# Second mix of a two-block kernel: convolved tiles interleaved with gate and decay tiles, convolution taps read from PSUM

## The chip, the cores and the metric

The kernel runs on one core of one Trainium2 chip. The metric is the device time of one execution in microseconds, as the median of several runs. Before the change it is 2250.25 us, the median of three runs (2248.23 to 2250.43). The profile is of another execution of the same program.

TensorE multiplies matrices into PSUM (PE in the profile; its weight loads are PEld). VectorE (DVE), ScalarE (ACT) and GpSimd (POOL) work element by element. SyncE (SP) starts the transfers of the weights.

## The reference, cut to what matters

Two blocks follow one another on a sequence of 256 tokens of width 1024. Each is a mixing layer and a lookup among 16384 single-neuron experts. The change lies in the mixing layer of the second block. There one projection `proj = h @ w_in` feeds two recurrences:

```python
qkv = causal_conv_silu(concat(a_q, a_k, a_v), conv_a)        # 4 taps along the tokens, then x * sigmoid(x)
o_a = gated_delta_rule(q, k, v, sigmoid(a_beta), log_alpha)  # 8 heads, chunks of 64 tokens
y_a = (rmsnorm(o_a) * silu(a_gate)) @ w_branch_a
f   = lb + (1 - lb) * sigmoid(b_f)                           # decay
o_b = hgrn2(silu(b_q), 1 - f, b_i, log(f))
y_b = (rmsnorm(o_b) * sigmoid(b_gate)) @ w_branch_b
x   = x + (sigmoid(g_a) * y_a + sigmoid(g_b) * y_b) @ w_out
```

## The kernel before, in words

The projection of the second mix is cut into 80 tiles of 128 channels by 256 tokens. Each tile has its own 512 KB of weights. Weights pass through a ring: SP loads `raw`; ACT rounds it to `hi` (`_conv`, line 152); `lo = raw - hi` is formed by DVE for the first `lo_cut` of 1024 columns and by POOL for the others (line 157). A tile is then 24 matmuls of 128 x 256 (`tile_ch`, line 187), three for each of eight slices of the width: hi by x's high part, hi by its low part, lo by its high part. They add up in one of two PSUM buffers called `mm`. `CUT2 = [384, 640]` gives `lo_cut`: 384 for the first 24 tiles, 640 behind them.

The order of the tiles before is: 24 convolved tiles (for each of 8 heads q, k, v), 8 gate tiles (`a_gate`, written to `sga`), 8 decay tiles (`b_f`, to `fs`), 8 of `b_q` (to `qb`), 8 of `b_gate`, 8 of `b_i`, and 16 for the two mixing gates. Below, tiles count from 0, so the first 40 are tiles 0 to 39.

A convolved tile takes these steps (`conv`, lines 1006 to 1017): ACT copies `mm` to `cvx` (1009), which frees `mm`; ACT makes `cva` from it, scaled by the fourth tap (1011); DVE adds the three other taps, 128 x 255, 254 and 253, with a shift of one to three tokens (1013); ACT takes the sigmoid `cvs` (914); DVE multiplies (1017). Then PE transposes the product (`head`, 1025), and ACT takes sums of squares and copies.

Behind the tiles run generators, which the tile loop advances by two rounds a tile (`after(2)`): `columns` (lines 918 to 1003) makes the decay matrices; `delta(0)` and then `delta(1)` compute the gated delta rule for four heads each; `chain` does the other recurrence (`hgrn`). In `delta`, products on PE (1075) give two matrices; `blocks16` inverts 16 x 16 blocks in a ladder of 15 steps of two DVE instructions (1237, 1238) and writes `X` (1251); three levels follow, each of products on PE (1093, 1094), a mask on DVE (1100), copies on ACT (1104), a product on PE (1110) and a subtraction on DVE (1113); several products end in a transposition (1201) and a product with the gate (1204). Of `hgrn`, the products on DVE are lines 1316 and 1317 and a masked copy is line 1334. Generators take PSUM from six named banks, `y0` to `y3`, `g0` and `g1`, kept in a queue `free` (`bank`, `need`, `done`).

Each engine carries out its instructions in the order in which they stand in its own queue. When the program is built, the framework orders the recorded instructions on each engine by a timeline that it models, so the order on an engine is not simply that of the Python code.

## Time and profile before

| | us |
|---|---|
| median of three runs | 2250.25 (2248.23 to 2250.43) |
| the profiled execution | 2248.88 |
| its span, first to last instruction | 2247.1 |
| PE busy in the span | 2181.1 (97%) |
| DVE busy | 1546.5 (69%) |
| ACT busy | 1166.4 (52%) |
| POOL busy | 829.3 (37%) |

The shares of the whole span say little about one stage. The rows that follow are therefore taken from stretches of the second mix, which starts at about 964 us. Windows give the busy time of each engine in a stretch with the number of its instructions; waits give who waited for whom; the rows of a line give the shortest, median and longest of its instructions. A matmul's record overlaps the next one's, so a count of matmuls in a stretch where PE is never idle gives PE's pace, and their durations do not. A matmul of full 32-bit numbers, as in lines 1025, 1075, 1093 and 1201, stands as two records. A few per cent of the matmul records can be missing.

### The profile page before, as it was taken

How to read it: one execution, taken by the hardware profiler on the slowest of the kernel's cores; microseconds unless marked ns; L12 is line 12 of the kernel's file. 1: busy time of each engine (PE TensorE's matmuls, PEld its weight loads, DVE VectorE, ACT ScalarE, POOL GpSimd, SP SyncE). 2: the span in 40 equal slices, each digit the busy share in tenths (PEclk: the TensorE clock that was granted, in tenths of full speed). 3: DMA queues.
4: the chain of work that ended last, by engine and by line, in shares of the span. 5: the costliest groups of instructions: out<-in, count | busy, mean ns of one | idle time of the engine just before them, and what ended most of it. 6: DMA issues, size and time to landing. Idle time of an engine off the chain costs nothing. (4 is left out here: it accounts for less than half of the span.)

```text
span 2247.1 us, 41435 instructions
## 1 busy us (share of the span) xinstructions
PE 2181.1 (97%) x15512; PEld 2025.8 (90%) x15512; DVE 1546.5 (69%) x3119; ACT 1166.4 (52%) x2210; POOL 829.3 (37%) x626
## 2 busy tenths in 40 slices
PE   8999999999999999988899999999999999999998
PEld 7989999999988888778899898899999999888887
DVE  5659986889544544579756787799778885454444
ACT  5645545444555555565444555455454445555554
POOL 3454000000166666645553675530000001656664
PEclk9999999999999999999999999999999999999999
DMA  5555655555556666633334244555555555666664
GB/s 187 158 172 167 183 174 162 159 160 160 178 191 202 205 191 196 187 101 119 123 104 136 64 132 140 178 165 185 171 168 154 157 160 180 195 204 191 195 195 153
DMA packets 103881, 370.90 MB, mean 165 GB/s; under 512 B 12928, under 2 KB 14080, under 8 KB 103424
## 3 DMA queue, kind: packets, MB, share of 16 engines
q1 hardware_dynamic: 101808, 365.21, 52.1%
q10 hardware_dynamic: 1872, 3.04, 0.4%
q8 instruction: 122, 2.00, 0.4%
q14 instruction: 79, 0.65, 0.1%
HBM read 367.16 MB, written 1.05 MB: 164 GB/s over the span
## 5 line engine op out<-in xcount | busy, mean ns | idle before, releaser
L157 POOL TENSOR_TENSOR lo<-raw,hi 128x384 fp32r<-128x384 f32 (+2 forms) x428 | 702.3, 1643 | 1337.3 <-ACT hi L152 1306.7
L152 ACT ACTIVATE hi<-raw 128x1024 fp32r<-128x1024 f32 x684 | 724.0, 1060 | 693.6 <-PE mm L187 405.9
L187 PE MATMUL mm<-xh,hi 128*128 128x256 f32 x3168 | 918.8, 290 | 15.5 <-ACT cvx L1009 5.7
L187 PE MATMUL mm<-xh,lo 128*128 128x256 f32 x3168 | 902.8, 285 | 0.4 <-DVE lo L157 0.4
L187 PE MATMUL mm<-xl,hi 128*128 128x256 f32 x3168 | 898.8, 284 | 1.3 <-DVE xl L309 1.0
L157 DVE TENSOR_TENSOR lo<-raw,hi 128x640 fp32r<-128x640 f32 (+2 forms) x654 | 665.9, 1019 | 336.1 <-ACT hi L152 331.8
L187 PEld LDWEIGHTS mm<-xh,hi 128*128 128x128 f32 x3168 | 603.4, 190 | 19.6 <-ACT cvx L1009 6.8
L187 PEld LDWEIGHTS mm<-xl,hi 128*128 128x128 f32 x3168 | 604.0, 191 | 2.7 <-DVE xl L309 1.6
L187 PEld LDWEIGHTS mm<-xh,lo 128*128 128x128 f32 x3168 | 599.8, 189 | 0.6 <-DVE lo L157 0.6
L261 PE MATMUL y<-lo,ah 128*128 128x512 f32 x1024 | 398.3, 389 | 0.0
L261 PE MATMUL y<-hi,ah 128*128 128x512 f32 x1024 | 397.4, 389 | 0.0
L261 PE MATMUL y<-hi,al 128*128 128x512 f32 x1024 | 276.0, 389 | 0.0
L617 DVE TENSOR_TENSOR al<-a,ah 128x256 fp32r<-128x256 f32 x256 | 118.7, 464 | 188.8 <-PE y L261 188.5
L261 PEld LDWEIGHTS y<-lo,ah 128*128 128x128 f32 x1024 | 192.2, 188 | 40.2 <-POOL lo L157 0.3
L261 PEld LDWEIGHTS y<-hi,al 128*128 128x128 f32 x1024 | 192.2, 188 | 39.8
L261 PEld LDWEIGHTS y<-hi,ah 128*128 128x128 f32 x1024 | 192.2, 188 | 39.8
L616 ACT ACTIVATE ah<-a 128x256 fp32r<-128x256 f32 x256 | 106.4, 416 | 167.2 <-PE y L261 165.7
L517 DVE TENSOR_TENSOR ow<-ow,w 128x1024 f16<-128x1024 f16 x128 | 87.3, 684 | 0.1
L545 ACT ACTIVATE a<-mm 128x256 f32<-128x256 f32 (+33 forms) x228 | 69.2, 303 | 0.0
L527 PEld LDWEIGHTS <-o 128*128 128x128 f16 x1024 | 59.6, 97 | 6.3
L514 DVE TENSOR_TENSOR ow<-iota,ij 128x1024 f16<-128x1024 f16 x64 | 44.3, 692 | 27.6 <-PE by L527 19.1
L533 DVE TENSOR_TENSOR a<-by,a 128x256 f32<-128x256 f32 (+15 forms) x144 | 47.8, 349 | 11.9 <-PE by L527 11.6
(500 smaller groups left out, 1972.1 us busy)
## 6 DMA issues: line engine op xcount, KB each, us to landing
raw<-in_u_dram SPq DMA_DIRECT2D x256, 512.0 KB, 3.6
raw<-in_v_dram SPq DMA_DIRECT2D x256, 512.0 KB, 4.2
raw<-in_w_in_dram SPq DMA_DIRECT2D x108, 512.0 KB, 3.6
raw<-in_wq_dram SPq DMA_DIRECT2D x32, 512.0 KB, 3.9
raw<-in_w_out_dram SPq DMA_DIRECT2D x16, 512.0 KB, 3.6
raw<-in_w_branch_a_dram SPq DMA_DIRECT2D x8, 512.0 KB, 3.5
raw<-in_w_branch_b_dram SPq DMA_DIRECT2D x8, 512.0 KB, 3.7
skT<-in_sk_dram ACTq DMA_DIRECT2D x2, 1024.0 KB, 5.2
```

What stands on the lines that cost most here:

```text
L152: self.nc.scalar.activation(out=h, in_=r, func=ACTF.Copy)
L157: eng.tensor_tensor(out=l[:, a:b], in0=r[:, a:b], in1=h[:, a:b].bitcast(F32), op=ALU.subtract)
L187: self.nc.tensor.matmul(out=ps, lhsT=a[:, c, :], rhs=b, start=(c == 0 and k == 0), stop=(c == NC - 1 and k == 2))
L261: i = self.nc.tensor.matmul(out=self.y[tt][dh], lhsT=p[:, ts], rhs=q[:, ds], start=(first and m == 0), stop=(last and m == 2))
L514: nc.vector.tensor_tensor(out=ow[0], in0=iota, in1=some(self.ij[:, 1]), op=ALU.is_equal)
L517: nc.vector.tensor_tensor(out=ow[q], in0=ow[0], in1=some(self.w[:, q]), op=ALU.mult)
L527: nc.tensor.matmul(out=g[:, n, :], lhsT=hot[n][0], rhs=hot[n][1 + q], start=(q == 0), stop=(q == 1))
L533: nc.vector.tensor_tensor(out=v, in0=gi[:, e:e + hi - lo], in1=v, op=ALU.mult)
L545: nc.scalar.activation(out=a[:, s, n:T], in_=ps[:, n:T], func=ACTF.Gelu)
L616: nc.scalar.activation(out=h, in_=a, func=ACTF.Copy)
L617: nc.vector.tensor_tensor(out=l, in0=a, in1=h.bitcast(F32), op=ALU.subtract)
```

## The change

The first 40 tiles come in another order: up to the twelfth convolved tile, one gate tile follows each three convolved tiles, and then one gate or decay tile follows each convolved tile. The columns of the weights are laid out to match. A convolved, gate or `b_q` tile takes one of the six named banks for its sums (`tile_wide`, named `wm`) if four or more are free when it is recorded, and otherwise `mm` as before. The copy `cvx` goes: ACT makes `cva` from PSUM, and DVE's three taps read PSUM. The sigmoid and the product of a tile are recorded two rounds later, one tile, in `head`. `lo_cut` is 640 from the first tile. `delta` waits for the heads that it needs by name, has two more rounds behind `blocks16`, and `columns` has three more rounds in one place.

```diff
+    def tile_wide(self):
+
+        if len(self.free) < 4:
+            return self.tile_ch(), lambda: None
+        tag = self.free.popleft()
+        return self.tile_ch(tag=tag), lambda: self.done(tag)
+
...
-    def tile_ch(self, xh=None, xl=None):
+    def tile_ch(self, xh=None, xl=None, tag=None):
...
-        ps = self.ps.tile([P, T], F32, tag="mm", name="mm", bufs=2)
+        if tag is None:
+            ps = self.ps.tile([P, T], F32, tag="mm", name="mm", bufs=2)
+        else:
+            ps = self.ps.tile([P, T], F32, tag=tag, name="wm")
...
-CUT2 = [384, 640]
+CUT2 = [640, 640]
...
-        yield
+        for _ in range(4):
+            yield
         nc.vector.tensor_scalar(out=self.beta, in0=eb, scalar1=1.0, scalar2=None, op0=ALU.add)
...
-    def conv(self, ps, n, out):
+    def conv(self, h, what):
+
         k, nc = self.k, self.k.nc
-        c = self.t([P, T], "cvx", tag="hon", bufs=2)
-        nc.scalar.activation(out=c, in_=ps, func=ACTF.Copy)
+        n = what * 8 + h
+        ps, done = k.tile_wide()
         a = self.t([P, T], "cva", tag="c0", bufs=3)
-        nc.scalar.activation(out=a, in_=c, func=ACTF.Copy, scale=self.cw[:, n, 3:4])
+        nc.scalar.activation(out=a, in_=ps, func=ACTF.Copy, scale=self.cw[:, n, 3:4])
         for s in (1, 2, 3):
-            nc.vector.scalar_tensor_tensor(out=a[:, s:T], in0=c[:, 0:T - s], scalar=self.cw[:, n, 3 - s:4 - s], in1=a[:, s:T],
+            nc.vector.scalar_tensor_tensor(out=a[:, s:T], in0=ps[:, 0:T - s], scalar=self.cw[:, n, 3 - s:4 - s], in1=a[:, s:T],
                                            op0=ALU.mult, op1=ALU.add)
+        done()
+        k.spawn(self.head(h, what, a))
+
+    def head(self, h, what, a):
+        k, nc = self.k, self.k.nc
+        yield
+        yield
         s = self.t([P, T], "cvs", tag="c1", bufs=2)
         self.sigmoid(s, a)
-        nc.vector.tensor_tensor(out=out, in0=a, in1=s, op=ALU.mult)
-
-    def head(self, h, what, src):
-
-        k, nc = self.k, self.k.nc
+        src = self.t([P, T], "vc", tag="vc", bufs=2) if what == 2 else (self.qc, self.kc)[what][:, h, :]
+        nc.vector.tensor_tensor(out=src, in0=a, in1=s, op=ALU.mult)
+        yield
         yield from k.need(1)
...
         k.done(bt)
+        self.ready.add(("head", h, what))
...
         ss = self.ssq[g4]
+        while not all(("head", h, what) in self.ready for h in hs for what in range(3)):
+            yield
...
         yield from self.blocks16(lt, X)
+        yield
+        yield
...
-        for h in range(H):
-            for what in range(3):
+        for kind, h, what in mix2_in_order():
+            if kind == "c":
+                self.conv(h, what)
+            elif kind == "a":
+                ps, done = k.tile_wide()
+                silu(ps, self.sga[:, h, :], oa)
+                done()
+            else:
                 ps = k.tile_ch()
-                dst = self.t([P, T], "vc", tag="vc", bufs=2) if what == 2 else (self.qc, self.kc)[what][:, h, :]
-                self.conv(ps, what * 8 + h, dst)
-                k.spawn(self.head(h, what, dst))
-                after(2)
-            if h == 3:
+                self.sigmoid(self.fs[:, h, :], ps)
+            after(2)
+            if (kind, h, what) == ("c", 3, 2):
                 k.spawn(self.both())
...
         for h in range(H):
-            ps = k.tile_ch()
+            ps, done = k.tile_wide()
             silu(ps, self.qb[:, h, :])
+            done()
             after(2)
...
+def mix2_in_order():
+
+    conv = [("c", h, what) for h in range(H) for what in range(3)]
+    rest = [("a", h, 0) for h in range(H)] + [("f", h, 0) for h in range(H)]
+    for n, c in enumerate(conv):
+        yield c
+        if n % 3 == 2 or n >= 12:
+            yield rest.pop(0)
```

The orders below are of the built programs. The first place is DVE's queue in the run of convolved tiles (`cva` is a tile in the making, `qc`, `kc` and `vc` the finished q, k and v). Before:

```order
L1013 SCALAR_TENSOR_TENSOR cva_11632<-cvx_11630,i_conv_a_2_932,cva_11632 128x255
L1013 SCALAR_TENSOR_TENSOR cva_11632<-cvx_11630,i_conv_a_2_932,cva_11632 128x254
L1013 SCALAR_TENSOR_TENSOR cva_11632<-cvx_11630,i_conv_a_2_932,cva_11632 128x253
L157 TENSOR_TENSOR lo_11765<-raw_11603,hi_11763 128x384
L1017 TENSOR_TENSOR kc_11011<-cva_11632,cvs_11637 128x256
L1013 SCALAR_TENSOR_TENSOR cva_11682<-cvx_11680,i_conv_a_2_932,cva_11682 128x255
L1013 SCALAR_TENSOR_TENSOR cva_11682<-cvx_11680,i_conv_a_2_932,cva_11682 128x254
L1013 SCALAR_TENSOR_TENSOR cva_11682<-cvx_11680,i_conv_a_2_932,cva_11682 128x253
L157 TENSOR_TENSOR lo_11825<-raw_11652,hi_11823 128x384
L1017 TENSOR_TENSOR vc_11679<-cva_11682,cvs_11687 128x256
```

and now, where line 164 is the old 157, 1025 the taps and 1037 the product:

```order
L1025 SCALAR_TENSOR_TENSOR cva_11668<-wm_11643,i_conv_a_2_932,cva_11668 128x255
L1025 SCALAR_TENSOR_TENSOR cva_11668<-wm_11643,i_conv_a_2_932,cva_11668 128x254
L164 TENSOR_TENSOR lo_11719<-raw_11595,hi_11717 128x640
L1025 SCALAR_TENSOR_TENSOR cva_11668<-wm_11643,i_conv_a_2_932,cva_11668 128x253
L164 TENSOR_TENSOR lo_11765<-raw_11641,hi_11763 128x640
L1025 SCALAR_TENSOR_TENSOR cva_11706<-wm_11681,i_conv_a_2_932,cva_11706 128x255
L1037 TENSOR_TENSOR qc_11010<-cva_11668,cvs_11711 128x256
L1025 SCALAR_TENSOR_TENSOR cva_11706<-wm_11681,i_conv_a_2_932,cva_11706 128x254
L1025 SCALAR_TENSOR_TENSOR cva_11706<-wm_11681,i_conv_a_2_932,cva_11706 128x253
L164 TENSOR_TENSOR lo_11811<-raw_11679,hi_11809 128x640
```

A tile's three taps now read `wm`, its bank. Beside a convolved tile's `lo`, now of 640 columns, stands the `lo` of a gate tile. The product of a tile stands among the taps of the next one, where before it stood ahead of them.

The second place is ACT's queue for the same tiles (`hi` is the rounding, `cvs` the sigmoid). Before:

```order
L152 ACTIVATE hi_11763<-raw_11603 128x1024
L1009 ACTIVATE cvx_11680<-mm_11654 128x256
L914 ACTIVATE cvs_11637<-cva_11632 128x256
L1011 ACTIVATE cva_11682<-cvx_11680,i_conv_a_2_932 128x256
L1030 ACTIVATE sq_11595,ssq0_11008<-by0_11592 128x128 x2
L152 ACTIVATE hi_11823<-raw_11652 128x1024
L1009 ACTIVATE cvx_11726<-mm_11701 128x256
L914 ACTIVATE cvs_11687<-cva_11682 128x256
L1011 ACTIVATE cva_11728<-cvx_11726,i_conv_a_2_932 128x256
```

and now (159 is the old 152, 924 the old 914, 1050 a copy of `head`):

```order
L1023 ACTIVATE cva_11668<-wm_11643,i_conv_a_2_932 128x256
L159 ACTIVATE hi_11717<-raw_11595 128x1024
L1050 ACTIVATE vs_11012<-by3_11633 128x2x128
L159 ACTIVATE hi_11763<-raw_11641 128x1024
L1023 ACTIVATE cva_11706<-wm_11681,i_conv_a_2_932 128x256
L924 ACTIVATE cvs_11711<-cva_11668 128x256
L159 ACTIVATE hi_11809<-raw_11679 128x1024
L1023 ACTIVATE cva_11749<-wm_11724,i_conv_a_2_932 128x256
L924 ACTIVATE cvs_11757<-cva_11706 128x256
```

One copy a tile is gone. The sigmoid of a tile stands where it stood before: behind a `hi` and the next tile's first read of its sums, which before was `cvx` and now is `cva`.

The third place is DVE's queue in the ladder of `delta(1)` (`svm` and `svY` are the ladder's two instructions a step, `hz` is a product of `hgrn`). Before:

```order
L1237 TENSOR_TENSOR svm_13173<-svL_13118,svY_13119 128x2x6x6
L1238 TENSOR_REDUCE svY_13119<-svm_13173 128x2x6
L157 TENSOR_TENSOR lo_13636<-raw_13493,hi_13634 128x640
L1237 TENSOR_TENSOR svm_13209<-svL_13118,svY_13119 128x2x7x7
L1418 TENSOR_TENSOR qb_11016<-mm_13550,ss_13575 128x256
L1238 TENSOR_REDUCE svY_13119<-svm_13209 128x2x7
L1237 TENSOR_TENSOR svm_13212<-svL_13118,svY_13119 128x2x8x8
L1238 TENSOR_REDUCE svY_13119<-svm_13212 128x2x8
L1237 TENSOR_TENSOR svm_13215<-svL_13118,svY_13119 128x2x9x9
```

and now (1259 and 1260 are the ladder, 1311, 1338 and 1339 the products of `hgrn`):

```order
L1259 TENSOR_TENSOR svm_13403<-svL_13346,svY_13347 128x2x6x6
L1260 TENSOR_REDUCE svY_13347<-svm_13403 128x2x6
L1311 TENSOR_TENSOR hz_13578<-hz_13578,hk_13510 128x128
L1259 TENSOR_TENSOR svm_13441<-svL_13346,svY_13347 128x2x7x7
L1260 TENSOR_REDUCE svY_13347<-svm_13441 128x2x7
L1338 TENSOR_TENSOR hz_13623<-hz_13623,hk_13503 128x2x64
L1339 TENSOR_TENSOR hz_13623<-hz_13623,qb_11016 128x2x64
L1259 TENSOR_TENSOR svm_13444<-svL_13346,svY_13347 128x2x8x8
L1260 TENSOR_REDUCE svY_13347<-svm_13444 128x2x8
L164 TENSOR_TENSOR lo_13665<-raw_13464,hi_13663 128x640
```

The ladder's steps now share the queue with products of `hgrn`, which before stood almost all behind the three levels.

## Rows read from the trace of the kernel before

**Rows 1.** Windows: us; busy us (instructions) of PE, PEld, DVE, ACT, POOL; granted clock; DMA

```profile
964.00:995.00 31.00, 27.14 (x217) 25.00 (x215) 25.45 (x53) 21.46 (x46) 15.24 (x13) 1.00 0.47 142
964.00:1101.00 137.00, 115.10 (x869) 110.27 (x868) 125.55 (x234) 81.82 (x201) 72.68 (x51) 0.93 0.40 121
1101.00:1161.00 60.00, 60.00 (x513) 58.27 (x511) 21.87 (x32) 24.03 (x38) 25.05 (x20) 1.00 0.34 105
1161.00:1240.00 79.00, 73.58 (x593) 70.40 (x592) 53.13 (x94) 35.70 (x64) 37.88 (x33) 0.98 0.41 128
1240.00:1283.00 43.00, 38.09 (x305) 36.60 (x303) 32.62 (x87) 25.18 (x70) 27.91 (x49) 0.92 0.20 62
```

**Rows 2.** Waits of PE, 964 to 1101 us: us in total, times, longest

```profile
PE by L1025 <- DVE kc L1017: 6.3, 5, 4.1
PE bg L1025 <- DVE vc L1017: 5.8, 3, 3.3
PE mm L187 <- ACT cvx L1009: 5.7, 4, 2.5
```

**Rows 3.** Waits of ACT, 964 to 1101 us, the longest in total

```profile
ACT cvs L914 <- DVE cva L1013: 31.7, 15, 4.8
```

**Rows 4.** Lines 1013, 1420, 1009: ns min/median/max, first and last start us, forms

```profile
L1013 DVE SCALAR_TENSOR_TENSOR cva<-cvx,i_conv_a,cva x72: 388/480/1885, 971.1 to 1082.4; 128x255 f32<-128x255 f32 x24, 128x254 f32<-128x254 f32 x24, 128x253 f32<-128x253 f32 x24
L1420 DVE SCALAR_TENSOR_TENSOR sga<-mm,i_a_onorm,ss x8: 471/477/479, 1084.0 to 1112.5; 128x256 f32<-128x256 f32 x8
L1009 ACT ACTIVATE cvx<-mm x24: 361/370/396, 968.6 to 1076.3; 128x256 f32<-128x256 f32 x24
```

**Rows 5.** Timeline at 1046 and 1097 us, DVE beside POOL: start, us, instruction

```profile
1046.66 1.82 DVE L1013 SCALAR_TENSOR_TENSOR cva<-cvx,i_conv_a,cva 128x255 f32<-128x255 f32 x1
1046.63 1.56 POOL L157 TENSOR_TENSOR lo<-raw,hi 128x640 fp32r<-128x640 f32 x1 [1.84 <-ACT hi L152]
...
1097.23 0.47 DVE L1420 SCALAR_TENSOR_TENSOR sga<-mm,i_a_onorm,ss 128x256 f32<-128x256 f32 x1
1097.28 1.00 POOL L157 TENSOR_TENSOR lo<-raw,hi 128x384 fp32r<-128x384 f32 x1 [0.65 <-ACT hi L152]
```

**Rows 6.** DVE groups by form, 964 to 1101 us: busy us, mean ns, idle before

```profile
L157 DVE TENSOR_TENSOR lo<-raw,hi 128x384 fp32r<-128x384 f32 x23 | 19.7, 858 | 1.7 <-ACT hi L152 1.6
L157 DVE TENSOR_TENSOR lo<-raw,hi 128x640 fp32r<-128x640 f32 x8 | 7.9, 985 | 1.1 <-ACT hi L152 1.0
L1420 DVE SCALAR_TENSOR_TENSOR sga<-mm,i_a_onorm,ss 128x256 f32<-128x256 f32 x5 | 2.4, 476 | 0.0
L1055 DVE TENSOR_SCALAR rr<-rr 128x8 f32<-128x8 f32 x2 | 2.0, 992 | 0.0
L1052 DVE TENSOR_TENSOR irk<-ssq,rr 128x8 f32<-128x8 f32 x2 | 2.0, 988 | 0.6 <-POOL rr L1047 0.6
```

**Rows 7.** Window of line 1013 alone: us, DVE busy us (instructions)

```profile
964.00:1101.00 137.00, 51.38 (x72) 0.93 0.40 121
```

**Rows 8.** Window of line 1017 alone

```profile
964.00:1101.00 137.00, 13.30 (x24) 0.93 0.40 121
```

**Rows 9.** Lines 1093 and 1201: ns min/median/max, first and last start us

```profile
L1093 PE MATMUL bg<-X,decc x64: 218/246/275, 1100.7 to 1217.9; 128*128 128x64 f32 x48, 128*64 128x64 f32 x16
L1201 PE MATMUL by<-k_ident,decc x12: 271/273/273, 1160.6 to 1260.3; 128*128 128x128 f32 x12
```

**Rows 10.** Lines 1104 and 1113

```profile
L1104 ACT ACTIVATE XTp<-by x10: 578/598/600, 1102.1 to 1228.3; 128x512 f32<-128x512 f32 x7, 64x512 f32<-64x512 f32 x3
L1113 DVE TENSOR_TENSOR X<-X,by x5: 674/686/689, 1108.3 to 1223.2; 128x512 f32<-128x512 f32 x5
```

**Rows 11.** Lines 1316, 1317 and 1334

```profile
L1316 DVE TENSOR_TENSOR hz<-hz,hk x56: 277/410/1106, 1195.5 to 1357.8; 128x128 f32<-128x128 f32 x56
L1317 DVE TENSOR_TENSOR hz<-hz,qb x56: 272/282/1108, 1195.7 to 1358.5; 128x128 f32<-128x128 f32 x56
L1334 DVE COPY_PREDICATED fs<-k_lev_h,by x34: 280/294/449, 1246.7 to 1359.7; 128x128 f32<-128x128 int32 x34
```

## The prediction

> **What bounds the kernel now.** I read the windows first, to see in which stretch of the second mix PE stands. The reader is to see the count of matmuls beside the length. From 1101 to 1161 us PE never stands, and 513 records take 60 us, so a record takes 0.117 us [rows 1]. By that pace the 869 records from 964 to 1101 us (call it A) need 102 us and take 137, so 35 are lost [rows 1]. Six of these lie in the first 31 us, where 217 records would need 25 [rows 1]. The 60 us that follow (B) lose nothing. From 1161 to 1283 us (C), 898 records need 105 of 122 us, so 17 are lost [rows 1].

> Next, DVE in A: it is busy for 125.6 of 137 us, ACT for 82 and POOL for 73 [rows 1]. So PE, with 102, is not the bound there; DVE is. The waits say the same: PE's named ones are for the products `kc` and `vc` on DVE and for the copy that frees `mm` [rows 2], and ACT waits 31.7 us for DVE's taps before it can take a sigmoid [rows 3].

> Last, what fills DVE. The 72 taps take 51.4 us [rows 7], 0.714 each, but their median is 0.480 and their longest 1.885 [rows 4]. The 17 us above the median are not work. The timeline shows one case: a tap that began beside POOL's `lo` took 1.82 us, about as long as that `lo`, while the same kind of instruction reading PSUM took 0.47 beside another POOL `lo` [rows 5]. The eight of line 1420, which read PSUM as the taps now will, lie between 0.471 and 0.479 [rows 4]. I take a tap from PSUM as 0.477. From both sides: 0.388, the shortest tap, and 0.714, the present mean with its hold-ups.

> **The change part by part: A.** The end of A is the first product of `delta(0)`'s levels, at 1100.7 us [rows 9]. The orders of the two programs give what stands ahead of that place. On DVE it is now 55 taps instead of 72, 32 `lo`, all of 640 columns, instead of 31, 17 products instead of 24, 8 gate products instead of 5, and without the second group's small instructions, half of lines 1052 and 1055. DVE's sum is then, in us:

> 125.6 now
> − 51.4 taps [rows 7] + 55 × 0.477 = 26.2
> − 27.6 for `lo` [rows 6] + 32 × 0.985 = 31.5
> − 13.3 products [rows 8] + 17 × 0.554 = 9.4
> − 2.4 gate products + 8 × 0.476 = 3.8 [rows 6]
> − 2.0 small ones [rows 6]
> = 99.8.

> The uncertain term is the `lo` of 640 columns, which reads SBUF twice and so is not freed from POOL. Its eight cases have a mean of 0.985 [rows 6]; 0.858, the mean of the narrower one, gives 27.5 and a sum of 95.8. At the other end all 17 us of hold-ups come back on `lo`, and the sum is 117. I take 0.985, the row of the same shape.

> PE up to that place has ten records more in the order, 879, thus 103 us. So DVE no longer binds: 100 against 103. What PE still loses is not zero, since the two are equal and dependences remain. I keep the 6 us of the start, where the decay matrices and the first tiles' chain are as they were, and a quarter of the other 29, together 14. The quarter is a choice; its bounds are nothing and 14 (half). A then takes 117 us instead of 137, 20 less. [...]

> On ACT the 24 copies go, 24 × 0.370 = 8.9 us [rows 4]. Since ACT is busy for 82 of 137 us, I cost this at nothing by itself. What it might have shortened, the freeing of `mm` behind a busy ACT (5.7 us of PE's waits [rows 2]), is taken over by the taps: a bank is now held until DVE's third tap has read it. That is the added wait. Behind it on PE are the transpositions and `delta`'s products that want a bank, but a tile takes one only where four are free, so two of six or more are left for those; its cover is the tiles in `mm`, since decay tiles still go there. I cost it at nothing, at most the 5.7 us that the present waits for `cvx` cost.

> The sigmoid a tile later removes the wait of ACT for `cva`; the product then comes later too, and with it the transpositions of line 1025. These wait 12.1 us for `kc` and `vc` now [rows 2]. In the order they now stand behind about a tile's 24 matmuls more, 2.8 us at PE's pace, which covers the sigmoid and the product. That is part of the three quarters of 29 which I let go.

> **B and C.** B runs from the first product of line 1093 (1100.7 us) to the first of line 1201 (1160.6) [rows 9]. By the order it holds 17 program matmuls fewer than before, 396 for 413: a tile and some products have gone, while products of heads have come in. In records of the trace that is 480 for 513, or 56 us. Two of the steps of the levels now stand without a tile between them, so that in one a subtraction of 0.69 and in the other a mask, which I take as long, and two copies of 0.60 [rows 10] are bare: 2.6 us, estimated at 4 with the hand-overs between engines. That gives 60 us, as now. The 23 records that A and B together no longer carry (ten more, 33 fewer) come later and cost 23 × 0.117 = 2.7 us there. Net: 20 − 2.7 = 17 to 18 us.

> C holds `delta(1)`. The order puts 14 pairs of `hgrn`'s products and 12 masked copies more on DVE between its two ends. At medians (0.410 + 0.282, and 0.294 [rows 11]) that is 9.7 + 3.5 = 13.2 us; DVE is idle for 79 − 53.1 = 25.9 us between 1161 and 1240 [rows 1], so they fit, and what has moved ahead is missing later. I cost it at nothing. At the longest (1.106 + 1.108, and 0.449) it is 31.0 + 5.4 = 36.4, which exceeds the idle time by 10.5. The other way, more work on PE in this stretch can fill part of its 17 lost us, which I leave as a gain of up to 10. The added rounds in `columns` and `delta` move instructions in the order and issue none; SP's transfers of weights are the same in number and size, and the DMA share in A is 0.40 [rows 1], so a faster A leaves them room.

> The sum is made against the profiled execution, 2248.88 us, 1.4 below the median of 2250.25. Less 18 that is 2231; I add nothing for the 1.4, which is within the spread of the three runs.

> [...] The taps read 0.480 from SBUF at the median and a like instruction 0.477 from PSUM [rows 4], so the source makes no difference there. [...]

> **The rivals.** First, DVE stays the bound: the hold-ups move from the taps to `lo` and the products, which read SBUF twice. For it: `lo` is wider and its mean already differs by only 0.127 for 256 more columns, so hold-ups are in both. Against it: each hold-up needs POOL busy, and POOL's share shrinks from 640 to 384 columns of a tile. DVE then needs 117 us, keeps the 11.4 us in which it is idle now, and A takes 128: 8.7 less, 6 with the 2.7 given back, so 2243 (2239 to 2246).

> Second, more is gained: A loses only the 6 us of the start (109 us, 28 less), and C fills part of its 17. With 8 there it is 2249 − 28 + 2.7 − 8 = 2216 (2208 to 2222). For it: DVE and ACT then have slack everywhere, and the clock stays up. Against it: DVE and PE need nearly the same time in A, so each delay of either shows.

> Third, nothing is gained: A is faster by 5 to 10, and B and C give it back, in that `delta` starts earlier in the stream and meets the same chain with fewer tiles to cover it. 2246 to 2254.8.

> Fourth, slower: in C the ladder and the levels of `delta(1)` queue on DVE behind `hgrn`'s products, which POOL holds up. The place is the queue of line 1259. Its price is up to 36 us at the longest durations, and it decides once it is above the 18 gained, thus if most of the 14 pairs take over 0.6 us an instruction and nothing covers them: 2255 to 2265. Against it: the medians of the two products are about a third of their longest [rows 11].

> That the change does not do what it says I exclude: in the order all 24 convolved tiles stand in `wm`, and only decay tiles of the first 40 in `mm`.

> **How the numbers follow.** The forecast 2231, its own range 2222 to 2239: 0.48. DVE stays the bound: 0.20. More is gained: 0.17. Given back: 0.07. Slower: 0.08. A measurement of this kernel can tell about 0.2%, 4.5 us, from no change, so "same" is 2245.7 to 2254.8. Faster is 0.48 + 0.20 + 0.17 = 0.85, same 0.07, slower 0.08. The range takes in all of the first two and most of the third: 2213 to 2246. Outside it stay the lower third of "more" and the last two cases, 0.2 together.

> **What would show it.** In the profile of the changed kernel, the levels' first product (now on another line) comes at 1081 us if A takes 117 us. The taps have a median near 0.48 and none above 0.6; if long ones remain, the reading of the hold-ups is wrong. ACT's wait of 31.7 us for the taps is gone. PE's clock in A is nearer 1.00. From there to the first transposition that was on line 1201 it takes 60 us. DVE's busy time up to that first product is about 100 us; if it is 115 or more, the first rival holds. A ladder of `delta(1)` with steps over 1 us would show the fourth. The forecast is wrong if A takes more than 128 us or if C grows by more than 5.

## The result, and the profile after

The changed kernel takes 2224.48 us, the median of four runs (2220.53 to 2226.17), beside 2250.34 for the kernel before. The ratio is 0.9884, with a 95% interval of 0.9867 to 0.9901: 25.9 us less, where 19 had been forecast. The profiled execution took 2220.53 us, 28.35 less than that of before.

I measure all kernels here by one count. From 964 us to the first product with `w_out` each carries out about the same matmuls, 3105 to 3131 records, and at the pace of [rows 1], 0.117 us a record, they need some 365 us. (A transposition, as in lines 1025 and 1201 of the kernel before, stands as one record: the 24 convolved tiles leave 48 of line 1025 for their 48 transpositions. Only the other products of full 32-bit numbers stand as two: line 1075 leaves 64 for 32.) What a stretch takes beyond its records is lost time. A tile's matmuls alone begin 0.120 us apart at a granted clock of 1.00 (median of 617 steps in A of the kernel before; eight steps from 1185.83 to 1186.79 us), so some 3 us of what A loses are this pace, in all kernels alike. The windows of the kernel before are cut for this at the second group's first transposition (1260) and at the first product with `w_out` (1392). The columns are those of [rows 1]:

```profile
1161.00:1260.00 99.00, 89.70 (x707) 85.42 (x706) 67.90 (x141) 45.26 (x89) 49.52 (x58) 0.95 0.34 108
1260.00:1392.00 132.00, 126.06 (x1034) 121.11 (x1033) 103.56 (x222) 81.84 (x214) 95.58 (x132) 1.00 0.39 117
964.00:1392.00 428.00, 390.85 (x3115) 375.07 (x3114) 318.87 (x628) 232.95 (x541) 242.83 (x260) 0.96 0.37 114
```

And after, with the levels' first product at 1081 us, the first transposition at 1139, the second group's at 1254 and the first product with `w_out` at 1364:

```profile
964.00:1081.00 117.00, 107.41 (x866) 103.99 (x864) 96.16 (x204) 67.84 (x151) 57.57 (x47) 0.99 0.48 147
1081.00:1139.00 58.00, 56.66 (x477) 54.58 (x478) 31.28 (x51) 28.31 (x61) 22.27 (x19) 1.00 0.29 92
1139.00:1254.00 115.00, 111.06 (x926) 107.90 (x925) 90.95 (x195) 59.54 (x134) 71.76 (x94) 0.99 0.35 110
1254.00:1364.00 110.00, 103.75 (x843) 99.22 (x843) 88.74 (x176) 66.81 (x172) 78.43 (x102) 1.00 0.39 125
964.00:1364.00 400.00, 378.87 (x3107) 365.69 (x3106) 307.13 (x623) 222.50 (x516) 230.03 (x259) 0.99 0.39 122
```

The first two stretches answer to the second and third row of [rows 1]. A takes 117 us for 866 records and loses 117 − 101 = 16 us, where 35 were lost. B takes 58 and loses 2. C, up to the second group's transposition, holds 926 records instead of 707 and loses 7 instead of 16. D, the rest, loses 11 as before. Together 37 us are lost instead of 64. Of the 27 less, up to some 10 are the clock, an estimate. The profile shows a lower level, 0.50, at which a tile's matmuls begin 0.213 us apart (median of 61 steps in A of the kernel before; eleven from 1042.07 to 1044.42 us), so at most 0.44 of the time at that level is lost. Before, it held for 20.4 us of A (mean 0.93) and 10.3 of C (0.95), at most 9 and 4.5 us lost; now for 3.4 us of each (0.99), at most 1.5 each.

The taps and the two landmarks, which answer to [rows 4] and [rows 9] (line 1025 the taps, 1115 the levels, 1223 the transposition):

```profile
L1025 DVE SCALAR_TENSOR_TENSOR cva<-wm,i_conv_a,cva x72: 416/476/484, 969.2 to 1134.9; 128x255 f32<-128x255 f32 x24, 128x254 f32<-128x254 f32 x24, 128x253 f32<-128x253 f32 x24
...
L1115 PE MATMUL bg<-X,decc x64: 221/270/324, 1080.9 to 1216.3; 128*128 128x64 f32 x32, 128*64 128x64 f32 x32
...
L1223 PE MATMUL by<-k_ident,decc x8: 270/273/329, 1138.9 to 1255.4; 128*128 128x128 f32 x8
```

No tap is longer than 0.484 us now. DVE's groups up to the levels, which answer to [rows 6] (busy us, mean ns):

```profile
L164 DVE TENSOR_TENSOR lo<-raw,hi 128x640 fp32r<-128x640 f32 x32 | 29.6, 925 | 11.7 <-ACT hi L159 11.6
L1025 DVE SCALAR_TENSOR_TENSOR cva<-wm,i_conv_a,cva 128x255 f32<-128x255 f32 (+2 forms) x55 | 25.8, 473 | 1.7 <-ACT cva L1023 1.3
L1259 DVE TENSOR_TENSOR svm<-svL,svY 128x2 f32<-128x2 f32 (+14 forms) x15 | 7.2, 477 | 0.1
...
L1037 DVE TENSOR_TENSOR vc<-cva,cvs 128x256 f32<-128x256 f32 x6 | 4.0, 672 | 0.0
L1037 DVE TENSOR_TENSOR qc<-cva,cvs 128x256 f32<-128x256 f32 x6 | 3.8, 642 | 0.8 <-ACT cvs L924 0.8
...
L1037 DVE TENSOR_TENSOR kc<-cva,cvs 128x256 f32<-128x256 f32 x6 | 3.3, 546 | 0.0
```

And the waits for the taps, which answer to [rows 2, 3], of ACT and then of PE:

```profile
ACT cvs L924 <- DVE cva L1025: 3.9, 4, 1.7
```

```profile
PE wm L197 <- ACT sq L1047: 2.1, 2, 1.2
PE wm L197 <- DVE cva L1025: 1.8, 3, 0.8
PE by L1042 <- DVE qc L1037: 1.6, 2, 1.4
```

ACT's wait for the taps has gone from 31.7 to 3.9 us, and PE's waits are all small. What is left of hold-ups on DVE shows in the products, which read SBUF twice: 18 take 11.1 us, 0.617 each, where 24 took 0.554 each before [rows 8]. Eight of the 18 took 0.84 to 1.12 us, each beside a POOL `lo` or product of `delta`, and ended 0.28 to 0.29 us after it; the others took 0.36 to 0.46. It shows too in the ladder's first instruction, which also reads SBUF twice: 15 take 7.2 us, 0.477 each, where they took 0.371 before. Four of them took 0.56 to 0.96 us beside a POOL `lo`; the steps next to these took 0.18 to 0.35. Before:

```profile
L1237 DVE TENSOR_TENSOR svm<-svL,svY 128x2 f32<-128x2 f32 (+14 forms) x15 | 5.6, 371 | 0.1
```

In C, PE's longest wait before and after:

```profile
PE mm L187 <- DVE qb L1418: 3.9, 3, 3.3
```

```profile
PE by L1115 <- DVE X L1273: 1.4, 1, 1.4
```

The 3.9 us for `qb` are gone; and the clock's mean is 0.99 for 0.95, at most 1.5 us lost for 4.5; in the second profile it is 0.97, and 3.

### The profile page after: what moved, and what is told of

Read it like the earlier page. It is cut to its first block, busy times and chain, and to the rows that moved or that the text cites. A ratio compares the mean times of both kernels' runs of the same rounds, so it can differ in the third digit from the quotient of the medians.

```text
span 2218.7 us, 41397 instructions
## 1 busy us (share of the span) xinstructions
PE 2168.3 (98%) x15512; PEld 2016.1 (91%) x15512; DVE 1534.3 (69%) x3119; ACT 1156.9 (52%) x2185; POOL 819.9 (37%) x626
## 5 line engine op out<-in xcount | busy, mean ns | idle before, releaser
L164 POOL TENSOR_TENSOR lo<-raw,hi 128x384 fp32r<-128x384 f32 (+1 forms) x428 | 690.7, 1616 | 1308.3 <-ACT hi L159 1272.0
L164 DVE TENSOR_TENSOR lo<-raw,hi 128x640 fp32r<-128x640 f32 (+1 forms) x654 | 666.1, 1019 | 309.0 <-ACT hi L159 301.6
L197 PE MATMUL mm<-xh,hi 128*128 128x256 f32 x2848 | 821.6, 288 | 5.1 <-DVE sg L861 2.5
L197 PE MATMUL mm<-xh,lo 128*128 128x256 f32 x2848 | 808.1, 284 | 0.5 <-DVE lo L164 0.4
L197 PE MATMUL mm<-xl,hi 128*128 128x256 f32 x2848 | 803.8, 282 | 1.0 <-DVE xl L319 0.7
L197 PEld LDWEIGHTS mm<-xh,hi 128*128 128x128 f32 x2848 | 537.4, 189 | 7.0 <-DVE sg L861 3.0
L197 PEld LDWEIGHTS mm<-xh,lo 128*128 128x128 f32 x2848 | 534.3, 188 | 0.9 <-DVE lo L164 0.9
L197 PE MATMUL wm<-xh,hi 128*128 128x256 f32 x320 | 92.9, 291 | 5.5 <-ACT sq L1047 2.1
L197 PE MATMUL wm<-xh,lo 128*128 128x256 f32 x320 | 91.4, 287 | 0.6 <-DVE lo L164 0.6
L197 PE MATMUL wm<-xl,hi 128*128 128x256 f32 x320 | 91.5, 286 | 0.1
```

The costliest lines, as they stand in the source:

```text
L164: eng.tensor_tensor(out=l[:, a:b], in0=r[:, a:b], in1=h[:, a:b].bitcast(F32), op=ALU.subtract)
L197: self.nc.tensor.matmul(out=ps, lhsT=a[:, c, :], rhs=b, start=(c == 0 and k == 0), stop=(c == NC - 1 and k == 2))
```

## The experiments

Lost time in us, by the windows of each kernel's own landmarks (length less records × 0.117), with the mean granted clock of A and of B. A ratio is to the kernel before as it was measured beside that run, at 2248.8 to 2249.1 us:

| kernel | median us | ratio to before [95%] | A | B | C | D | clock A, B |
|---|---|---|---|---|---|---|---|
| before | 2250.3 | 1 | 35 | 0 | 16 | 11 | 0.93, 1.00 |
| changed, again | 2224.8 | 0.989 [0.987, 0.991] | 16 | 2 | 9 | 11 | 0.99, 1.00 |
| taps from SBUF | 2236.3 | 0.994 [0.993, 0.995] | 22 | 4 | 15 | 11 | 0.97, 0.97 |
| old order | 2225.9 | 0.989 [0.988, 0.991] | 26 | 2 | 4 | 9 | 0.94, 1.00 |
| before, taps from PSUM | 2240.3 | 0.996 [0.995, 0.997] | 36 | 0 | 9 | 10 | 0.93, 1.00 |
| no named banks | 2232.7 | 0.993 [0.992, 0.994] | 24 | 0 | 16 | 9 | 0.96, 1.00 |
| no delay | 2235.4 | 0.995 [0.993, 0.996] | 20 | 10 | 9 | 11 | 0.97, 0.87 |
| `b_q` in `mm` | 2228.3 | 0.991 [0.989, 0.992] | 19 | 2 | 10 | 11 | 0.96, 1.00 |
| before, PSUM and banks | 2236.5 | 0.994 [0.992, 0.995] | 32 | 3 | 6 | 9 | 0.92, 0.97 |
| no added rounds | 2234.5 | 0.993 [0.992, 0.995] | 22 | 7 | 9 | 10 | 0.96, 0.92 |
| `lo` cut at 384 | 2239.7 | 0.996 [0.995, 0.997] | 28 | 1 | 16 | 9 | 0.93, 1.00 |
| `lo` all on DVE | 2237.6 | 0.995 [0.994, 0.996] | 21 | 9 | 12 | 11 | 0.96, 0.89 |

The theory was that of the prediction: POOL's `lo` holds up DVE's taps, and with that gone DVE no longer binds A. The rivals were that the order does it, that the banks do it, or that the later sigmoid does. Most runs undo one part of the change; two do one or two parts alone, and three set the columns of `lo` otherwise.

**The changed kernel again.**

> The changed kernel as it is, beside the three other kernels on the same chip. All theories: 2221 to 2227 us, 23 to 30 us less than before.

2224.8, as expected. The same kernel's two profiles differ by 2.6 us of lost time in all, so a smaller difference in one profile tells nothing.

**The taps read SBUF.** The edit:

```diff
+        c = self.t([P, T], "cvx", tag="hon", bufs=2)
+        nc.scalar.activation(out=c, in_=ps, func=ACTF.Copy)
+        done()
...
-            nc.vector.scalar_tensor_tensor(out=a[:, s:T], in0=ps[:, 0:T - s], ...
+            nc.vector.scalar_tensor_tensor(out=a[:, s:T], in0=c[:, 0:T - s], ...
```

> The changed kernel, but with the copy of each convolved tile to SBUF again, and the taps read the copy. Theory of the taps (POOL's lo holds up instructions that read SBUF, and that filled DVE): the mean of a tap goes back from 0.47 to about 0.71 us, so the 55 taps ahead of the levels cost 13 us more, DVE's sum there goes from 96 to 109 us, above PE's 103; the time is 5 to 12 us above the changed kernel's, 2229 to 2236. Theory of the order (what counts is that a third fewer convolved tiles stand ahead of the levels): within 3 us of the changed kernel.

11.6 us above the changed kernel, at the upper end. The line of the taps, the window of A, and two taps with the POOL piece beside them:

```profile
L1028 DVE SCALAR_TENSOR_TENSOR cva<-cvx,i_conv_a,cva x72: 420/482/1278, 972.1 to 1147.4; 128x255 f32<-128x255 f32 x24, 128x254 f32<-128x254 f32 x24, 128x253 f32<-128x253 f32 x24
```

```profile
964.00:1090.00 126.00, 111.56 (x888) 107.98 (x887) 108.71 (x210) 75.07 (x172) 59.86 (x48) 0.97 0.46 139
```

```profile
1000.23 1.79 DVE L1028 SCALAR_TENSOR_TENSOR cva<-cvx,i_conv_a,cva 128x254 f32<-128x254 f32 x2
...
1000.75 1.00 POOL L164 TENSOR_TENSOR lo<-raw,hi 128x384 fp32r<-128x384 f32 x1 [1.23 <-DVE cva L1028]
```

The mean of a tap went back to 0.63, less than the 0.71 expected; POOL's piece is shorter now (1.00 us here, 1.56 in [rows 5]). DVE is busy for 108.7 us in A, as the theory had it (109). The two taps took 1.79 us together, about 0.8 more than two of 0.48, and ended at 1002.02, 0.27 us after POOL's `lo`, which began beside the second. Three taps from 1013.55 us on took 2.78 us together and ended at 1016.33, 0.28 us after another `lo`. The edit also puts 24 copies back on ACT; what they cost by themselves the next run tells.

**The taps read SBUF, `lo` all on DVE.** The edit, beside that of the last run:

```diff
-CUT2 = [640, 640]
+CUT2 = [1024, 640]
```

> As the run with the taps from SBUF, and with all 1024 columns of lo on DVE for the first 40 tiles, so that POOL forms none there. If POOL's lo is what holds the taps up, they lie between 0.39 and 0.50 us with a mean below 0.49 although they read SBUF, but lo costs 1.2 to 1.3 us each: DVE's sum up to the levels 100 to 106 us, the time 2222 to 2236. If the source itself makes them slow, long taps remain and the mean stays near 0.7.

2227.9 us, one execution only, so it is not in the table (A loses 18 us, B 4, C 7, D 12). The taps have a mean of 0.50 and four stay long; expected was none above 0.50. The line, and one of the four with what POOL did:

```profile
L1028 DVE SCALAR_TENSOR_TENSOR cva<-cvx,i_conv_a,cva x72: 422/478/1261, 972.1 to 1144.6; 128x255 f32<-128x255 f32 x24, 128x254 f32<-128x254 f32 x24, 128x253 f32<-128x253 f32 x24
```

```profile
1141.90 1.26 DVE L1028 SCALAR_TENSOR_TENSOR cva<-cvx,i_conv_a,cva 128x255 f32<-128x255 f32 x1
...
1141.66 1.22 POOL L1089 TENSOR_TENSOR kt<-kt,kg 128x512 f32<-128x512 f32 x1
```

POOL forms no `lo` for these tiles. The tap shown stands beside a product of `delta` (`kt`); two others of the four, at 1041.19 (1.26 us) and 1042.98 (0.65), stand beside the product `decc`, in two pieces from 1040.15 to 1043.35. So it is not `lo` alone: POOL's products hold a tap that reads SBUF too. The tap shown ended at 1143.16 us, 0.28 after the POOL instruction that began before it. With POOL's `lo` gone, the kernel with the copy and the taps from SBUF is about as fast as the changed one: neither the source nor the copy costs anything by itself.

**Only the source, in the kernel before.** The copy `cvx` goes and the taps read `mm`:

```diff
-        c = self.t([P, T], "cvx", tag="hon", bufs=2)
-        nc.scalar.activation(out=c, in_=ps, func=ACTF.Copy)
```

> The kernel before, with nothing changed but that the copy goes and cva and the taps read the sums in PSUM, in the two mm buffers. Theory of the taps: DVE needs about 17 us less in the stretch up to the levels, and 8 to 14 us are gained: 2236 to 2242. Theory of the banks (the two mm buffers are held by the taps, and PE waits for them): no gain or a loss, 2248 to 2265, with PE's waits for the taps of 10 us or more in that stretch.

2240.3: 8.8 us gained on the kernel before beside it (2249.1), as the first theory said, but with the wait that the second named. A and PE's longest wait in it:

```profile
964.00:1081.00 117.00, 91.22 (x696) 86.72 (x695) 96.60 (x207) 62.84 (x149) 57.46 (x39) 0.93 0.37 114
```

```profile
PE mm L187 <- DVE cva L1011: 16.5, 8, 9.3
```

DVE falls to 96.6 us, as in the changed kernel, and the levels begin at 1081 as there. Yet A loses 36 us as before: only 696 records fit into it. DVE has time to spare, but the two buffers are now held by the taps and PE waits 16.5 us for them. What is gained is gained in C, where 824 records now stand for 707. A landmark that comes 20 us earlier is not 20 us gained.

**No named banks.** In `tile_wide` the condition is always true:

```diff
-        if len(self.free) < 4:
+        if True:
```

> The changed kernel, but every tile takes one of the two mm buffers, none a named bank. Theory of the banks: the taps hold the two buffers and PE waits for them, 2235 to 2250, with PE's waits for cva and taps of 8 us or more up to the levels. Theory of the taps alone: within 4 us of the changed kernel, 2221 to 2229.

7.9 us above the changed kernel, below the range of the theory of the banks and above that of its rival; the wait is the one it named:

```profile
PE mm L197 <- DVE cva L1025: 10.5, 8, 4.1
```

**The source and the banks, in the kernel before.** The edit of the fourth run, and `tile_wide` for the convolved tiles alone:

```diff
-                ps = k.tile_ch()
+                ps, done = k.tile_wide()
...
                 self.conv(ps, what * 8 + h, dst)
+                done()
```

> The kernel before with the taps reading PSUM (as in the run of that part alone, 2240), and the convolved tiles in named banks where four or more are free; order, delay, columns of lo, rounds and the other tiles as before. Theory of the pair (the source takes the hold-ups off DVE, but in two mm buffers PE then waits 16.5 us for the taps; banks take that wait away): 2228 to 2235, PE's waits for cva up to the levels under 4 us. Theory that banks matter only with the new order or the delay: 2237 to 2243.

2236.5, between the two ranges: 1.5 above that of the pair and 0.5 below that of its rival. PE's wait for `cva` is gone, as the first said, but others took its place:

```profile
PE mm L197 <- ACT cvs L924: 5.6, 1, 5.6
PE wm L197 <- DVE dec L1085: 4.8, 1, 4.8
PE wm L197 <- DVE cva L1021: 0.6, 1, 0.6
```

```profile
ACT cvs L924 <- DVE cva L1021: 12.5, 6, 3.9
ACT L924 <- DVE cva L1021: 3.7, 1, 3.7
```

ACT, in the old recording, still waits for the taps of the tile just done before it takes the sigmoid, 16.2 us in all, and PE for the sigmoid. A loses 32 us. So the banks add 4 us to the 9 of the source, and the two together give some 12 of the 24 us by which the changed kernel was faster in its second measurement.

**No delay of sigmoid and product; no added rounds.** Two runs. In the first the sigmoid and the product are recorded with the taps, and `head` has none of its three rounds; in the second:

```diff
-        for _ in range(4):
-            yield
+        yield
...
         yield from self.blocks16(lt, X)
-        yield
-        yield
```

> The changed kernel, but a convolved tile's sigmoid and product are recorded with its taps, not a tile later. If the delay matters, ACT waits again for the taps (31.7 us before, 3.9 now) and 4 to 8 us are lost: 2228 to 2233. If DVE's load was all, within 3 us of the changed kernel.

> The changed kernel without the three added rounds in columns and the two behind blocks16. My prediction held these at nothing: 2221 to 2228. Theory from the run without delay (there the levels of the first group stood bare between 1100 and 1115 us and PE's clock was at half): what fills the levels is set by the rounds, and the same stretch of half clock appears: 2230 to 2237.

2235.4 and 2234.5, each some 10 us above the changed kernel; the first is above the range expected, the second in that of the second theory. ACT's waits for the taps return only in part without the delay (10.6 us in two groups); A loses 20 and 22 us. The rest is new and lies in B, 8 and 5 us, where no wait of PE is longer than 0.8 us in either run. Slices of 5 us in the levels, without the delay and then in the changed kernel (second profile; its slice from 1095 to 1100, busy throughout at 1.00, is not shown), the first of each being the one in which PE last stood idle for long:

```profile
1095.00:1100.00 5.00, 3.69 (x29) 3.00 (x28) 1.76 (x3) 1.61 (x6) 1.23 (x1) 0.93 0.40 105
1100.00:1105.00 5.00, 5.00 (x21) 2.80 (x20) 0.00 (x0) 0.59 (x1) 0.00 (x0) 0.50 0.00 0
1105.00:1110.00 5.00, 4.67 (x21) 4.24 (x21) 0.00 (x0) 1.07 (x2) 0.00 (x0) 0.50 0.02 3
1110.00:1115.00 5.00, 5.00 (x23) 4.66 (x23) 0.69 (x1) 0.00 (x0) 0.00 (x0) 0.50 0.00 0
```

```profile
1090.00:1095.00 5.00, 3.65 (x35) 3.31 (x34) 1.62 (x3) 1.47 (x3) 1.18 (x1) 1.00 0.31 105
1100.00:1105.00 5.00, 5.00 (x37) 3.88 (x37) 2.21 (x5) 3.14 (x10) 1.64 (x1) 1.00 0.37 105
1105.00:1110.00 5.00, 5.00 (x43) 4.79 (x42) 1.09 (x2) 2.06 (x6) 0.00 (x0) 1.00 0.00 0
1110.00:1115.00 5.00, 5.00 (x44) 5.00 (x44) 2.27 (x4) 2.85 (x6) 1.66 (x1) 1.00 0.11 24
```

Behind that slice PE is busy in both, but for 0.3 us. Without the delay it runs at the lower level from 1100 to 1115 us and carries out 21 to 23 records in 5 us, the changed kernel 37 to 44 at the higher. Without the rounds the same happens from about 1102 to 1112. The timelines differ in what follows the waits. Without the delay, PE goes from its wait for `X` straight on to the third level's products:

```profile
1096.55 1.97 PE L1129 MATMUL by<-pm,XTp 128*128 128x64 f32 x16 [0.76 <-ACT XTp L1123]
1098.35 0.39 PE L1039 MATMUL by<-k_ident,qc 128*128 128x128 f32 x2
1099.30 0.47 PE L1112 MATMUL bg<-X,decc 128*64 128x64 f32 x2 [0.55 <-DVE X L1132]
```

So it does without the rounds, after waits of 0.76 and 0.56 us. In the changed kernel a tile's 24 matmuls stand between, from 1096.08 us on:

```profile
1096.08 0.37 PE L197 MATMUL wm<-xh,hi 128*128 128x256 f32 x1
```

So rounds that issue no instruction are worth 10 us here. They move the tiles among the levels; that the missing tile is what lets the clock fall fits both runs, but no run tests it alone.

**The old order of the tiles.** 24 convolved tiles, then 8 and 8, all else as changed:

```diff
-    for n, c in enumerate(conv):
-        yield c
-        if n % 3 == 2 or n >= 12:
-            yield rest.pop(0)
+    yield from conv
+    yield from rest
```

> The changed kernel, but with the tiles in the order of before (24 convolved, 8 gate, 8 decay). Theory of the taps: 69 taps stand ahead of the levels, at 0.477, DVE's sum there is about 100 us, and most of the gain stays: 2226 to 2236. Theory of the order: the gain is gone, 2242 or more.

2225.9: no difference from the changed kernel (2224.8), 0.1 below the first theory's range. A and C:

```profile
964.00:1076.00 112.00, 95.01 (x734) 90.83 (x734) 93.61 (x211) 64.05 (x157) 50.46 (x41) 0.94 0.42 129
1135.00:1260.00 125.00, 122.58 (x1038) 119.77 (x1037) 89.20 (x190) 65.58 (x142) 72.89 (x95) 1.00 0.39 121
```

The levels begin earlier still, at 1076, with 734 records done. A loses 26 us, ten more than with the new order, and C only 4. What the order gives in A it takes back in C.

**The tiles of `b_q` in `mm`.**

```diff
-            ps, done = k.tile_wide()
+            ps = k.tile_ch()
             silu(ps, self.qb[:, h, :])
-            done()
```

> The changed kernel, but the eight tiles of b_q take the mm buffers as before. Theory that the later gain (about 9 us behind the first transposition of the first group) comes from these tiles no longer waiting for DVE: PE waits for qb again (3.9 us before), the clock falls after it, and 4 to 9 us are lost, 2228 to 2234. Theory that it comes from the earlier start of the other recurrence, whose matmuls fill PE: within 2 us of the changed kernel.

2228.3, at the lower end of the first theory's range, but only 3.6 above the changed kernel, with overlapping intervals. The wait came back, 4.5 us once:

```profile
PE mm L197 <- DVE qb L1440: 4.5, 1, 4.5
```

C loses 10 us, beside 7 and 9 in the two profiles of the changed kernel. So these banks explain at most a small part of C's gain.

**The columns of `lo`.** All else as changed, 384 and 1024 for 640.

> The changed kernel with lo cut at 384 columns for the first 40 tiles, so POOL forms 640. If only the taps' source mattered: within 3 us of the changed kernel, the taps still 0.47 us each although POOL's pieces are longer. If POOL's longer pieces hold up lo and products instead (the mean product goes from 0.62 to 0.8 us or more) or lo comes late to PE: 2228 to 2236.

> The changed kernel with all columns of lo on DVE for the first 40 tiles. A lo then takes 1.25 us instead of 0.93 (32 of them: 10 us more on DVE up to the levels), the products fall from 0.62 to 0.42 (3.5 us less): DVE 103 us there, about PE's need. If DVE still has slack: 2221 to 2228; if DVE binds again: 2229 to 2236.

2239.7 and 2237.6: both cost 13 to 15 us, more than either expectation. With 384 the taps stay at 0.47, and against the second expectation so do the products: 18 take 11.1 us, 0.62 each, as in the changed kernel. The ladder's first instruction takes longer, 0.678 us each. A, the ladder, and PE's two longest waits:

```profile
964.00:1093.00 129.00, 112.28 (x861) 108.56 (x860) 106.07 (x207) 67.84 (x149) 67.39 (x46) 0.93 0.42 129
```

```profile
L1259 DVE TENSOR_TENSOR svm<-svL,svY 128x2 f32<-128x2 f32 (+14 forms) x15 | 10.2, 678 | 0.2
```

```profile
PE wm L197 <- DVE sga L1442: 5.1, 1, 5.1
PE mm L197 <- DVE lo L164: 4.4, 2, 3.3
```

DVE is busy for 106 us, 10 more than with 640, though its 31 `lo` take 27.6 us and the 32 of 640 took 29.6: 3 of the 10 are the ladder, and the rest is spread over small instructions. PE waits for `sga` and `lo`; the clock of A is 0.93 again. With 1024, the window of A is:

```profile
964.00:1089.00 125.00, 113.05 (x888) 109.39 (x887) 98.79 (x209) 68.43 (x152) 16.71 (x16) 0.96 0.48 145
```

POOL is busy for 16.7 us and DVE for 98.8, not 103. DVE does not bind. The loss is in A (21), in C (12) and, as in the two runs without delay and without rounds, at the lower clock in B (9). The taps read PSUM here; with the taps from SBUF and the same `lo` it was 2227.9, in one execution. As far as one execution tells, the source pays only where POOL forms part of `lo`. Why this kernel is the slower of the two is not shown; the clock in B is half of the difference (B loses 9 us for 4).

## Why the prediction was right, and where it was off

**The mechanism of A was right.** The tap from PSUM took 0.473 us (0.477 forecast), DVE's sum up to the levels 96.2 us (99.8), PE's records 866 (879), the lost time 16 (14), the levels began at 1080.9 (1081). The runs with the taps from SBUF and with the source alone show both halves of it: POOL holds the taps up, and DVE's 125 us fall to 97 by the source alone. Not all of these 29 us are hold-ups: 20 are taps, of which 66 instead of 72 lie in that window, and 10 are seven `lo` that come later there. In the changed kernel the terms came out at 25.8 us for the taps (26.2), 29.6 for `lo` (31.5) and 11.1 for the products (9.4).

**Why the sum of A came out right is another matter.** I credited the 17 taps and 7 products that no longer stand ahead of the levels to the gain. With the old order 69 taps stand ahead, and the kernel is as fast. I charged the wider `lo` with 4 us; with the narrow one the kernel is 15 us slower. The source alone moved the landmark by 20 us and A still lost 36. The 20 us came from several parts, each of which removes the wait that the one before it leaves: the source (DVE's hold-ups), the banks (PE's 16.5 us for `cva`), the later sigmoid (ACT's 16.2 us for the taps). The step that a longer-held bank costs at most 5.7 us was right in the changed kernel (1.8 us), but only because the banks are there; without them it costs 8 us in time and 10.5 in waits. (A tile takes a bank only where four are free, so three are left for the others, not the two that I wrote.)

**The source by itself made no difference**, as I had read from [rows 4]: a tap took 0.476 us at the median from PSUM, 0.482 from SBUF in the run that undoes this part.

**The failed step is C, which I costed at nothing.** I had left it as a gain of up to 10 us in one direction and a loss in the other. It lost 16 us before and 7 to 9 after, and D 11 as before, though they take over the 39 records that A and B no longer hold (I had 23, and charged 2.7 us for them). The 9.6 us of the profiled pair are some 3 of the clock, an estimate from its means, and the rest waits, 3.9 of them for `qb`. That wait stood in the trace of before, and the diff moves just these tiles into named banks; I read the waits of A and not those of C. Had I taken 7 to 10 us for C, the forecast would have been 2221 to 2224. Among the other kernels C loses 4 to 16 us: least with the old order (clock 1.00), most where the clock's mean was 0.94 to 0.96. No single run accounts for it. B was close: 58 us for 477 records, where I had 60 for 480.

**A second step failed without showing in the sum:** the added rounds "move instructions in the order and issue none". Without them the kernel is 10 us slower. So are the source, the wider `lo`, the banks and the delay each worth 8 to 15 us given the rest, and with the rounds these values add up to 55 us, more than twice the gain: each part taken out lets another wait, or the lower clock, come back.

Of the rivals, the first (the hold-ups move to `lo` and the products) was true only of the products, 0.06 us on each of 18, and of the ladder, 0.1 us on each of 15; `lo` had a mean of 0.925, below the 0.985 taken. The second, more gained, came closest: its 8 us in C are about what came, while A lost 16 us and not 6. The third had B and C give the gain back, and both gained. Of the fourth, the sign that I had named, a step of `delta(1)`'s ladder over 1 us, came once (1.38 us, beside two of 1.27 before), and C lost less than before.

**Open.** Why the clock falls in the levels without the delay, without the rounds and with all `lo` on DVE, and not in the changed kernel, is not settled: there PE stands idle just as long shortly before (busy for 3.65 of 5 us, and 3.69 without the delay). Idle time alone does not tell. In C of the changed kernel the clock is at 0.50 too, from 1221.3 to 1224.7 us, and PE was busy throughout the 10 us before; in the last 8 of them it did only products of `delta(1)`'s last level and of `hgrn`, none of a tile. A change of any part also moves the order of all others. No version that was run is faster than the changed kernel beyond the noise, and the old order of the tiles equals it.

## What to carry to other kernels

When an instruction's mean is far above its median, look for the engine beside it before counting the instruction as work: here a third of the taps' time (17 of 51.4 us) was POOL, and reading PSUM removed it (no tap above 0.484 us). Then follow the buffer: here the taps held PSUM longer and needed more of it (PE waited 16.5 us for `cva` with two buffers, 0.6 with the banks), and the source alone gave 9 us, with more banks 12, of some 25; the rest came only with the other parts, of which the later use, the rounds and the wider `lo` are each worth some 10 us or more where all else is there. Judge a stretch by its records and its lost time, not by when a landmark comes.
